# Seven block products for eight in half of an FFN's down projection, summed in device memory, with gate and up products sharing PSUM banks

## The chip, the cores and the metric

The kernel runs on one core of one Trainium2 chip, in one launch. The metric is the time of one execution on the device in microseconds (us). Three runs of the kernel before gave 1963.62, 1964.08 and 1964.83 us; the median, 1964.08 us, is the time before.

## The reference, cut to what matters

One layer of a diffusion backbone on 384 tokens (128 context, 256 latent) of width 2048, in float32. The layer's last part, where the change lies, is a dense SwiGLU FFN with a hidden width of 5632:

```
h  = rmsnorm(x, norm_pre_ffn) * (1.0 + sc2) + sh2
ff = (silu(h @ w_ffn_gate) * (h @ w_ffn_up)) @ w_ffn_down
x  = x + ga2 * rmsnorm(ff, norm_post_ffn)
```

`sc2`, `sh2` and `ga2` come from a matrix `w_ada` of the conditioning vectors ("ada" below); the last sixth of it (for `ga2`) is worked out during the FFN.

## The kernel before, in words

**Number form.** Matrix products are made in float32 quality from two parts of each operand: `hi`, the operand rounded to float32r, and `lo`, the rest. A product is three matmuls: hi x hi, hi x lo, lo x hi. A weight tile of 128 x 1024 is loaded as it is (`raw`), ACT casts it to `whi` (L1398) and DVE subtracts to get `wlo` (L1409). Four buffers of each let this run three tiles ahead of PE.

**Chunks.** The hidden width is cut into 11 chunks of 512 (4 tiles of 128). Chunk 0 of gate and up is made with plain products. From chunk 1 on, gate and up together use a block scheme (Strassen's kind) over token tiles 1 and 2 (latent) and the two halves of the width 2048: sums of blocks of `h` are made once (`left_sums`, L1297), differences of weight tiles are made by DVE as they come (L1382, L1405, L1406, L1408), and ten results per chunk, `p1` to `p7` and `q1` to `q3`, are held in PSUM. They are reached by kinds of steps, four steps (i = 0..3) to a kind: A (p1, q1), B (p5, q3), C (q3, p3), E (p6), F (p7), G (q2, p2), H (p4) (`of_kind`, L1519). A step makes two products (12 matmuls of 128x512), or one (6) in E, F and H. `evict` (L1530) copies and adds the results into SBUF with ACT and DVE, applies SiLU, and multiplies to the hidden values. In each of the first three B steps of a chunk, one token tile of the hidden values of the chunk before is transposed on PE (`turn_hid`, L1553) into a PSUM tile `ptr`; from it ACT makes `hid_hi`, DVE `hid_lo`.

**Down projection.** The hidden values of chunk c - 1 are multiplied by w_d while chunk c's gate and up products run. A D step i takes one weight tile: columns 512 n of the output (n = i // 2) and half kh = i % 2 of the chunk, for three token tiles: 18 matmuls into three PSUM banks (`pdn`). After kh = 1, `out` (L1571) adds the three banks into `psums`, a running sum of 128 x 6144 in SBUF (for chunk 0 it copies).

**Order.** `steps` (L1320) is the written order of one chunk: A0-A3, B0-B3, then four times (C, E, D of n = 0, 1), then four times (F, G, H, D of n = 2, 3). At each step `grab2` (L1419) takes the next split weight tile, starts loads (`load_more`, L1361) and splits the tile three steps on (`split_next`, L1389). Work on results waits in two lists: `now`, run at the next step, and `pend`, of which three are run per step between ACT's cast and DVE's subtraction, or all of them before a D step that needs new banks. The tiles of A and B stay in eight slots (`slots`) since E, F and H use differences of them; the tiles of C, G and D come through two `raw` buffers. SP issues all these loads, in order.

**PSUM.** Five banks (`pss`) serve gate and up, taken in turn by the ten results (`banks`, L1513). Three banks (`psm`) serve `pdn`, `ptr` and the ada work's small tiles.

**Ada work.** `ada_last` (L1430) goes a step on after some A, G and late D steps (`paced`, at a rate of 0.85): a load and two scaled adds of 512 on DVE, and at the end of each of four quarters two small PE steps.

**The end.** The last D products go into `add_last` (L1566) and a closing part that norms, scales, transposes and writes the output.

Of the kernel before, what the change touches and what calls it, by code (L numbers as in the profile page):

```python
# [11 lines left out]
F32 = mybir.dt.float32  # L12
# [8 lines left out]
P = 128  # L21
# [75 lines left out]
def tile_step(ctx: ExitStack, tc: tile.TileContext, a, o):  # L97
# [947 lines left out]
    with ExitStack() as s:  # L1045
# [234 lines left out]
        psums = [actp.tile([P, 6, 512], F32, tag=t, name="psums") for t in ("B_hi", "B_lo")]  # L1280
# [4 lines left out]

        hid = hid_of()
        s_tiles = [pe.tile([P, 8, P], F32R, tag=f"S{n}", name="S", bufs=1) for n in range(2)]
        s_tiles += [pf.tile([P, 8, P], F32R, name=f"S{n}") for n in range(2, 6)]
# [8 lines left out]
        def left_sums():  # L1297

            raw = [psums[n // 3][:, 2 * (n % 3) : 2 * (n % 3) + 2, :].rearrange("p a (b c) -> p (a b) c", c=P) for n in range(4)]
# [21 lines left out]
        steps = []  # L1321
        for c in range(1, NFC):
            steps += [("A", c, i) for i in range(4)] + [("B", c, i) for i in range(4)]
            for i in range(4):
# [10 lines left out]
        def src_of(kind, c, i):  # L1335
            if kind == "D":
                return down_src(c, i // 2, i % 2)
            return gu_src(*{"A": ("u", c, 0), "B": ("g", c, 0), "C": ("g", c, 1), "G": ("u", c, 1)}[kind], i)

        entries = [["R", 0, 0, e[0]] for e in raws]  # L1340
# [5 lines left out]
        for kind, c, i in steps:  # L1346
            e = [kind, c, i, None]
            entries.append(e)
            if kind in "CGD":
                pairs.append((e, src_of(kind, c, i)))  # L1350
        resident = [(kind, c, i) for c in range(1, NFC) for kind in "AB" for i in range(4)]
        out_now = [sum(e[3] is not None for e in entries)]
        free = set(range(8))

        def slot(x, c, i):

            return 4 * ((c + x) % 2) + i

        def load_more(kept=1):
            while pairs and out_now[0] < 2:  # L1360
                e, src = pairs.pop(0)  # L1361
                e[3] = wp.tile([P, G], F32, tag="raw", name="raw", bufs=2)
                dst = e[3]
                if e[0] == "D":
                    dst = dst.rearrange("p (i x) -> p i x", i=2)
                elif e[0] != "R":
                    dst = dst.rearrange("p (n x) -> p n x", n=FC)
                SP.dma_start(dst, src)
                out_now[0] += 1
            while kept and resident:  # L1370
                kind, c, i = resident[0]
                k = slot(kind == "B", c, i)
                if k not in free:
                    return
                free.remove(k)
                SP.dma_start(slots[k].rearrange("p (n x) -> p n x", n=FC), src_of(kind, c, i))
                resident.pop(0)
                kept -= 1

        def sum1(c, i):  # L1380
            x, y = (slots[slot(n, c, i)] for n in range(2))
            DVE.tensor_sub(x, y, x)  # L1382
# [6 lines left out]
        def split_next():  # L1389

            if not entries:
                settle_pend()
                return
            kind, c, i, raw = entries.pop(0)
            x, y = (slots[slot(n, c, i)] if kind not in "RD" else None for n in range(2))
            src = raw if kind in "RCGD" else y if kind == "F" else x
            hi, lo = (wp.tile([P, G], F32R, tag=t, name=t, bufs=4) for t in ("whi", "wlo"))
            ACT.copy(hi, src)  # L1398
            settle_pend()
            if (kind, i) == ("A", 3):  # L1400
                sum1(c, 0)
            elif kind == "B" and i < 3:
                sum1(c, i + 1)
            elif kind == "C":
                DVE.tensor_sub(x, raw, x)  # L1405
                DVE.tensor_sub(y, raw, y)  # L1406
            elif kind == "G":
                DVE.tensor_sub(x, raw, x)  # L1408
            DVE.tensor_sub(lo, src, hi.bitcast(F32))  # L1409
            if kind in "RCGD":  # L1410
                out_now[0] -= 1
            elif kind == "F":
                free.add(slot(1, c, i))
            elif kind == "H":
                free.add(slot(0, c, i))
            ready.append((hi, lo))
# [73 lines left out]
        def products(w, todo, by_tile=False):  # L1490

            order = [(x, y) for x in ((0, 1),) for y in todo] if by_tile else [((0,), y) for y in todo] + [((1,), y) for y in todo]
            for ws, (dst, stat, mov, first, last) in order:
                for w_ in ws:
                    for m in range(2):
                        for x_ in range(2 - w_):
                            PE.matmul(  # L1497
                                dst, stat[x_][m], mov(w[w_], m),
                                start=first and w_ == m == x_ == 0, stop=last and w_ == m == 1,
                            )  # L1500
# [11 lines left out]

        def banks(c):  # L1513

            for n in ("p1", "q1", "p5", "q3", "p3", "p6", "p7", "p2", "q2", "p4"):
                bank[c, n] = pss.tile([P, 512], F32, tag="side", name="pgu")
# [13 lines left out]
        def evict(c, kind):  # L1530

            B = {n: bank[c, n] for n in ("p1", "q1", "p5", "q3", "p3", "p6", "p7", "p2", "q2", "p4")}
            add, mul = DVE.tensor_add, DVE.tensor_mul
            silu = lambda x: ACT.activation(x, x, AF.Silu)
            if kind == "A":
                now.extend([lambda: ACT.copy(s1, B["p1"]), lambda: ACT.copy(sq, B["q1"])])
            elif kind == "B":
                now.append(lambda: ACT.copy(s5, B["p5"]))
            elif kind == "C":
                pend.extend([lambda: add(g0, sq, B["q3"]), lambda: add(g1, s5, B["p3"]), lambda: silu(g0)])  # L1540
            elif kind == "E":
                pend.extend([lambda: add(e2, s1, B["p6"]), lambda: add(g1, g1, e2), lambda: silu(g1)])
            elif kind == "F":
                pend.extend([lambda: add(e2, e2, B["p7"]), lambda: add(s5, s5, e2), lambda: silu(s5)])
# [5 lines left out]
            elif kind == "H":  # L1550
                pend.extend([lambda: add(e2, e2, B["p4"]), lambda: mul(s5, s5, e2)])

        def turn_hid(dst, t, pool, tag):  # L1553
# [6 lines left out]
            pend.extend([lambda: ACT.copy(hi, pt), lambda: DVE.tensor_sub(lo, pt, hi.bitcast(F32))])  # L1560

# [18 lines left out]
        pd_tiles, hid_last, x1b, done = None, None, None, 0  # L1580
        for kind, c, i in steps:
# [8 lines left out]
            if kind == "D":  # L1590
                w = grab2()
                n, kh = i // 2, i % 2
                if kh == 0:
# [5 lines left out]
                    d_live[0] = 3  # L1599
# [6 lines left out]
                if kh == 1:  # L1606
                    if not last_c:
                        for t in range(3):
                            pend.append(lambda u=unit(t, n), p=pd_tiles[t], c=c: out(u, p, c))
# [11 lines left out]
                if (c, i) == (NFC - 2, 6):  # L1621
# [4 lines left out]
                    for t in range(3):  # L1626
                        turn_hid(hid_last, t, psm, "mm")
            else:
                if kind == "A" and i == 0:
                    banks(c)  # L1630
                w = grab2()
                products(w, [(bank[c, n], two_of(stat, i), mov_gu, first and i == 0, i == 3 and last) for n, stat, first, last in of_kind[kind]])
                if i == 3:
                    evict(c, kind)
                if kind == "B" and c > 1 and i < 3:

                    turn_hid(hid, i, psm, "mm")
# [157 lines left out]
```

## Time and profile before

| | |
|---|---|
| median of three runs | 1964.08 us (1963.62 to 1964.83) |
| profiled execution | 1964.35 us, of which its span 1962.6 us |
| matmuls of L1497 into `pgu`, `pdn` (128x512) | 2640 and 1584 |
| DVE adds into `psums`, chunks 1 to 9 | 108, median 680 ns |
| loads of w_d | 88 of 512 KB, 3.6 us to landing |
| bytes read from and written to device memory | 361 MB and 17 MB, 193 GB/s over the span |

How it is read: PE is the matrix engine, PEld its weight loads, DVE, ACT and POOL the vector, scalar and GpSimd engines, SP the engine that issues DMAs. A group line gives source line, engine, operation, output<-input by the program's names, shapes, count, and then busy time, the mean of one in ns, and the idle time of that engine just before. A stretch line gives the stretch, its length, the busy time and instruction count of PE, PEld, DVE, ACT and POOL, the granted clock of PE, the DMA share and GB/s. A line of the order in time gives start, duration and instruction, and in brackets the idle time before it and what ended it. A matmul's duration holds its passage through the array, so a chain of matmuls moves on faster than the sum of their durations.

### The profile page before, as it was taken

To read this page: it belongs to the slowest core of one execution; us is meant where nothing else is said; L and a number is where in the kernel's file an instruction comes from. 1 tells how busy PE (TensorE), PEld (TensorE's weight loads), DVE (VectorE), ACT (ScalarE), POOL (GpSimd) and SP (SyncE) were. 2 spreads that over 40 slices of the span, in tenths; PEclk is the share of its full clock that TensorE was granted. 3 is DMA by queue.
4 is the path that set the end of the run, shared out by engine and by line. 5 is a ranking of instruction groups with operands and counts; after the bars stand their busy time and mean duration, and the time that the engine had idled before them with its cause. 6 is when DMAs were issued, how large, how long until landed. Compare 5 with 4: busy or idle time off the path is not lost.

```text
span 1962.6 us, 27507 instructions
## 1 busy us (share of the span) xinstructions
PE 1946.2 (99%) x10576; PEld 1725.5 (88%) x10576; DVE 1629.0 (83%) x2075; ACT 908.0 (46%) x1281; POOL 32.2 (2%) x44
## 2 busy tenths in 40 slices
PE   8999999999999999999999999999999999999998
PEld 5779999999999999999988888888888888888886
DVE  5569888879866797977789998999898989887885
ACT  4233454544345654446455444444444444444444
POOL 0000000000000000004000000000000000000001
PEclk9999999999999999999999999999999999999999
DMA  9977677767754687655345445463636263625243
GB/s 389 370 261 269 222 247 237 234 219 251 255 201 148 228 261 237 217 163 213 112 145 173 160 134 170 142 195 122 194 121 208 95 216 105 202 72 193 75 161 129
DMA packets 189411, 380.06 MB, mean 194 GB/s; under 512 B 14172, under 2 KB 112668, under 8 KB 184928
## 3 DMA queue, kind: packets, MB, share of 16 engines
q1 hardware_dynamic: 189136, 377.92, 57.4%
q8 instruction: 83, 1.36, 0.3%
q14 instruction: 48, 0.39, 0.1%
q10 hardware_dynamic: 144, 0.39, 0.1%
HBM read 361.48 MB, written 16.78 MB: 193 GB/s over the span
## 4 chain that ended last, share of the span: by engine, by line
PE 95%; DMA 2%; DVE 2%; ACT 1%; issue 0%; SPq 0%; DVEq 0%; ACTq 0%
PE pmm L258 35%; PE pgu L1497 30%; PE pdn L1497 18%; PE pv L398 3%; PE pgm L381 1%; DMA slab<-in_w_ada 1%; PE pf L996 1%; PE px L416 1%; PE pmm L1251 1%; PE ptr L1558 1%; PE po L645 1%; PE pf L997 0%; DMA raw<-in_w_br_gla 0%; DMA raw<-in_w_d 0%; PE pr L580 0%
## 5 line engine op out<-in xcount | busy, mean ns | idle before, releaser
L258 PE MATMUL pmm<-A_hi,whi 128*128 128x384 f32 x1200 | 404.3, 337 | 0.0
L258 PE MATMUL pmm<-A_hi,wlo 128*128 128x384 f32 x1200 | 401.4, 334 | 0.0
L258 PE MATMUL pmm<-A_lo,whi 128*128 128x384 f32 x1200 | 401.3, 334 | 0.0
L1398 ACT CAST whi<-u 128x1024 fp32r<-128x1024 f32 x200 | 210.7, 1053 | 285.8 <-DVE u L1382 86.2
L224 ACT CAST whi<-raw 128x1024 fp32r<-128x1024 f32 x181 | 189.7, 1051 | 188.9 <-DMA raw<-in_w_gate 63.2
L1398 ACT CAST whi<-raw 128x1024 fp32r<-128x1024 f32 x175 | 184.2, 1052 | 198.3 <-PE pgu L1497 59.9
L1409 DVE TENSOR_TENSOR wlo<-u,whi 128x1024 fp32r<-128x1024 f32 x200 | 243.9, 1220 | 33.6 <-ACT whi L1398 18.6
L225 DVE TENSOR_TENSOR wlo<-raw,whi 128x1024 fp32r<-128x1024 f32 x179 | 218.1, 1221 | 57.9 <-ACT whi L224 57.2
L1497 PE MATMUL pgu<-whi,A_hi 128*128 128x512 f32 x640 | 250.0, 391 | 0.0
L1497 PE MATMUL pgu<-whi,A_lo 128*128 128x512 f32 x640 | 249.3, 389 | 0.0
L1409 DVE TENSOR_TENSOR wlo<-raw,whi 128x1024 fp32r<-128x1024 f32 x175 | 213.3, 1219 | 33.7 <-ACT whi L1398 21.9
L258 PEld LDWEIGHTS pmm<-A_hi,whi 128*128 128x128 f32 x1200 | 225.3, 188 | 2.9 <-issue 1.4
L258 PEld LDWEIGHTS pmm<-A_lo,whi 128*128 128x128 f32 x1200 | 225.4, 188 | 0.2
L258 PEld LDWEIGHTS pmm<-A_hi,wlo 128*128 128x128 f32 x1200 | 225.3, 188 | 0.0
L572 DVE SCALAR_TENSOR_TENSOR adacc<-adaw,spad,adacc 128x1024 f32<-128x1024 f32 x180 | 222.8, 1279 | 2.6 <-DMA adaw<-in_w_ada 2.2
L1497 PE MATMUL pdn<-whi,hid_hi 128*128 128x512 f32 x480 | 186.9, 389 | 0.0
L1497 PE MATMUL pdn<-whi,hid_lo 128*128 128x512 f32 x480 | 186.8, 389 | 0.0
L1497 PE MATMUL pgu<-wlo,A_hi 128*128 128x512 f32 x640 | 184.2, 389 | 0.0
L1497 PEld LDWEIGHTS pgu<-whi,A_hi 128*128 128x128 f32 x640 | 120.1, 188 | 26.1 <-issue 0.8
L1497 PEld LDWEIGHTS pgu<-wlo,A_hi 128*128 128x128 f32 x640 | 120.1, 188 | 25.4
L1497 PEld LDWEIGHTS pgu<-whi,A_lo 128*128 128x128 f32 x640 | 120.1, 188 | 25.0
L1497 PE MATMUL pgu<-whi,S 128*128 128x512 f32 x480 | 131.1, 395 | 0.0
(367 smaller groups left out, 2763.2 us busy)
## 6 DMA issues: line engine op xcount, KB each, us to landing
adaw<-in_w_ada SPq DMA_DIRECT2D x96, 512.0 KB, 4.3
raw<-in_w_d SPq DMA_DIRECT2D x88, 512.0 KB, 3.6
slab<-in_w_ada SPq DMA_DIRECT2D x32, 1024.0 KB
raw<-in_w_gate SPq DMA_DIRECT2D x64, 512.0 KB, 4.7
raw<-in_w_g SPq DMA_DIRECT2D x48, 512.0 KB, 3.3
raw<-in_w_u SPq DMA_DIRECT2D x48, 512.0 KB, 3.3
raw<-in_w_in SPq DMA_DIRECT2D x44, 512.0 KB, 4.4
u<-in_w_u SPq DMA_DIRECT2D x40, 512.0 KB, 4.9
```

The source lines that it names most:

```text
L224: ACT.copy(hi, raw)
L225: sub = lambda: eng.tensor_sub(lo, raw, hi.bitcast(F32))
L258: PE.matmul(dst, w[wi][:, k * n + n0 : k * n + n0 + P], x[xi][:, k0 + k, :], start=first and k == 0 and j == 0, stop=last and k == kts - 1 ...
L381: PE.matmul(pgv[q : q + 32, :], spad[:, k, :], slab[k // (KT // 2)][:, k % (KT // 2), :], start=k < 4, stop=k >= KT - 4,)
L398: PE.matmul(pv[2 * t + g], hT[x_][:, kb, t * P : (t + 1) * P], w_[:, g * 512 : (g + 1) * 512], start=kb == 0 and j == 0, stop=kb == KT - 1 ...
L416: PE.matmul(px, w_[:, u * P : (u + 1) * P], hT[x_][:, kb, :], start=j == 0, stop=j == 2)
L572: DVE.scalar_tensor_tensor(acc[:, c, :], w, spad[:, k, c : c + 1], acc[:, c, :], op0=ALU.mult, op1=ALU.add,)
L645: PE.matmul(dst, w[wi], x[xi], start=first and j == 0, stop=last and j == 2)
L996: PE.matmul(pf[:, 0 : 2 * HT], w[0][:, c], x[k], start=k == 0, stop=False)
L1398: ACT.copy(hi, src)
L1409: DVE.tensor_sub(lo, src, hi.bitcast(F32))
L1497: PE.matmul(dst, stat[x_][m], mov(w[w_], m), start=first and w_ == m == x_ == 0, stop=last and w_ == m == 1,)
```

## The change

For the columns n = 0, 1 of w_d and chunks 0 to 8, the four weight blocks (two n, two kh) are multiplied with the hidden values of token tiles 1 and 2 in seven block products instead of eight; token tile 0 keeps its four products. New steps: DA (q1, p1), DB (p5, q3), DC (q3, p3), DE (p6), DF (p7), DG (q2, p2), DH (p4). DA's and DB's weight tiles stay in two new slots; DVE makes four differences of weight tiles, and three more tiles have to be split. `hid_sums` makes four sums of blocks of the hidden values with DVE, reading the transposes in PSUM, and their hi and lo parts.

The ten results are not combined in each chunk: each is a sum over chunks kept in device memory (`sums_d`), and so are the six results of n = 2, 3. `to_sums` copies a bank with ACT into one of four SBUF buffers; SP writes it for chunk 0, and an accumulating DMA of POOL adds it for chunks 1 to 8. In the last chunk they are loaded back (`sums_back`, `sums_rest`), and nine adds (`sums_join`) combine them in `psums`. Chunk 9's down projection and the last one are as before.

The space of `psums` holds, until then, the two slots, the buffers and the hidden sums.

Gate and up: the ten results become chains in five fixed banks. Q is q1, copied after A and added to in B and C; X is p1 (A), then p6 (E), p7 (F) and p4 (H) added on top; Z is p5 (B), then p3 (C). X and Z change places from chunk to chunk. `evict` copies some sums out on the way and has seven adds or products to make instead of twelve. The order of a chunk is now A, B, four times (C, E, D-step), four times (F, G, D-step), four times (H, D-step), with eleven D-steps: D4, D5, DA, DB, DC, D6, D7, DE, DF, DG, DH.

```diff
+        sums_d = dram.tile([16, P, 512], F32, name="sums_d")
...
+            if c < LAST:
+                dd = iter([("D", c - 1, 4), ("D", c - 1, 5), ("DA", c - 1, 0), ("DB", c - 1, 0), ("DC", c - 1, 0),
+                           ("D", c - 1, 6), ("D", c - 1, 7)] + [("D" + k, c - 1, 0) for k in "EFGH"])
...
             for i in range(4):
-                steps += [("C", c, i), ("E", c, i), ("D", c - 1, i)]
+                steps += [("C", c, i), ("E", c, i)] + more()
             for i in range(4):
-                steps += [("F", c, i), ("G", c, i), ("H", c, i)] + ([("D", c - 1, 4 + i)] if c < NFC - 1 or i < 2 else [])
+                steps += [("F", c, i), ("G", c, i)] + more()
+            for i in range(4):
+                steps += [("H", c, i)] + more()
...
+            if kind == "DA":
+                DVE.tensor_sub(x, y, x)
...
         of_kind = {
-            "A": (("p1", Hx(1, 0), True, True), ("q1", Hx(0, 0), True, True)),
-            "B": (("p5", S1, True, True), ("q3", Hx(0, 0), True, False)),
-            "C": (("q3", Hx(0, 8), False, True), ("p3", S4, True, True)),
-            "E": (("p6", S2, True, True),),
-            "F": (("p7", S3, True, True),),
-            "G": (("q2", Hx(0, 8), True, True), ("p2", Hx(1, 8), True, True)),
-            "H": (("p4", Hx(2, 8), True, True),),
+            "A": (("Q", Hx(0, 0), True), ("X", Hx(1, 0), True)),
+            "B": (("Z", S1, True), ("Q", Hx(0, 0), False)),
+            "C": (("Q", Hx(0, 8), False), ("Z", S4, False)),
+            "E": (("X", S2, False),),
+            "F": (("X", S3, False),),
+            "G": (("q2", Hx(0, 8), True), ("p2", Hx(1, 8), True)),
+            "H": (("X", Hx(2, 8), False),),
         }
...
             elif kind == "C":
-                pend.extend([lambda: add(g0, sq, B["q3"]), lambda: add(g1, s5, B["p3"]), lambda: silu(g0)])
+                now.append(lambda: silu(g0, B["Q"]))
             elif kind == "E":
-                pend.extend([lambda: add(e2, s1, B["p6"]), lambda: add(g1, g1, e2), lambda: silu(g1)])
+                now.append(lambda: ACT.copy(e2, B["X"]))
+                pend.extend([lambda: add(g1, e2, B["Z"]), lambda: silu(g1)])
             elif kind == "F":
-                pend.extend([lambda: add(e2, e2, B["p7"]), lambda: add(s5, s5, e2), lambda: silu(s5)])
+                pend.extend([lambda: add(s5, s5, B["X"]), lambda: silu(s5)])
...
+        def hid_sums(h1, h2):
+
+            r, (hi, lo) = dt["raw"], dt["S"]
+            add, sub = DVE.tensor_add, DVE.tensor_sub
+            return [
+                lambda: ACT.copy(r[:, 3], h2[:, 0:2]),
+                lambda: add(r[:, 0], r[:, 3], h2[:, 2:4]), lambda: sub(r[:, 1], r[:, 0], h1[:, 0:2]),
+                lambda: sub(r[:, 2], h1[:, 2:4], r[:, 1]), lambda: sub(r[:, 3], h1[:, 0:2], r[:, 3]),
+                lambda: ACT.copy(hi, r), lambda: sub(lo, r, hi.bitcast(F32)),
+            ]
+        of_d = {
+            "DA": lambda: (("q1", Hd(0, 0), True, True), ("p1", Hd(1, 0), True, True)),
+            "DB": lambda: (("p5", Sd(0), True, True), ("q3", Hd(0, 0), True, False)),
+            "DC": lambda: (("q3", Hd(0, 1), False, True), ("p3", Sd(2), True, True)),
+            "DE": lambda: (("p6", Sd(1), True, True),),
+            "DF": lambda: (("p7", Sd(3), True, True),),
+            "DG": lambda: (("q2", Hd(0, 1), True, True), ("p2", Hd(1, 1), True, True)),
+            "DH": lambda: (("p4", Hd(2, 1), True, True),),
+        }
+        def to_sums(k, p, c):
+
+            u = dt["out"][turn[0] % 4]
+            turn[0] += 1
+            ACT.copy(u, p)
+            if c == 0:
+                SP.dma_start(sums_d[k], u)
+            else:
+                POOL.dma_start(sums_d[k], u, accum_op=ALU.add)
+            d_live[0] -= 1
...
-        def out(u, p, c):
-            if c == 0:
-                ACT.copy(u, p)
-            else:
-                DVE.tensor_add(u, u, p)
+        def out(u, p):
+            DVE.tensor_add(u, u, p)
             d_live[0] -= 1
...
+                    if c < LAST and i == 3:
+                        if c == 1:
+                            f = dt["full"]
+                            pend.append(lambda: DVE.tensor_add(f, hid[0][:, :, P:T].bitcast(F32), hid[1][:, :, P:T].bitcast(F32)))
+                            pend.extend(hid_sums(f[:, :, 0:P], f[:, :, P:]))
+                        else:
+                            pend.extend(hid_sums(*hid_pt[1:]))
```

More of the change, by code (lines that the diff above doesn't have):

```diff
@@ L1380, in sum1 @@
         def sum1(c, i):
[L1381 removed]
+            x, y = (slots[slot(n, "A", c, i)] for n in range(2))
             DVE.tensor_sub(x, y, x)
@@ L1492, in products @@
             order = [(x, y) for x in ((0, 1),) for y in todo] if by_tile else [((0,), y) for y in todo] + [((1,), y) for y in todo]
-            for ws, (dst, stat, mov, first, last) in order:
+            for ws, (dst, stat, mov, first, last, *more) in order:
                 for w_ in ws:
@@ L1627, in tile_step @@
                         turn_hid(hid_last, t, psm, "mm")
-            else:
-                if kind == "A" and i == 0:
-                    banks(c)
+            elif kind[0] == "D":
+                w = grab2()
+                while pend:
+                    pend.pop(0)()
+                todo = []
+                for n, stat, first, last in of_d[kind]():
+                    if first:
+                        d_bank[n] = psm.tile([P, 512], F32, tag="mm", name="pds")
+                        d_live[0] += 1
+                    todo.append((d_bank[n], stat, mov_d, first, last))
+                    if last:
+                        pend.append(lambda k=PROD.index(n), p=d_bank[n], c=c: to_sums(k, p, c))
+                products(w, todo, by_tile=kind in ("DB", "DC"))
+            else:
@@ L1631, in tile_step @@
                 w = grab2()
-                products(w, [(bank[c, n], two_of(stat, i), mov_gu, first and i == 0, i == 3 and last) for n, stat, first, last in of_kind[kind]])
+                if kind == "H" and i == 0:
+                    while pend:
+                        pend.pop(0)()
+                B = banks(c)
+                products(
+                    w, [(B[n], two_of(stat, i), mov_gu, first and i == 0, i == 3, not first) for n, stat, first in of_kind[kind]],
+                    by_tile=(kind, i) in (("A", 3), ("B", 0), ("B", 3), ("C", 0)),
+                )
```

144 lines of the change are left out of this document (105 added, 39 removed).

## The prediction

> **What bounds the kernel now.** I read the page first, then the busy time by stretch for the part that the change touches (the FFN chunks, 1062 to 1912 us), then the chain of work there.
>
> ```profile
> span 1962.6 us, 27507 instructions
> PE 1946.2 (99%) x10576; PEld 1725.5 (88%) x10576; DVE 1629.0 (83%) x2075; ACT 908.0 (46%) x1281; POOL 32.2 (2%) x44
> ```
> ```profile
> 1062.00:1912.00 850.00, 850.00 (x3858) 701.82 (x3857) 763.44 (x833) 383.94 (x414) 0.00 (x0) 1.00 0.45 148
> ```
> ```profile
> 1212.70:1307.10 94.40, 94.40 (x424) 78.14 (x423) 91.40 (x103) 42.56 (x46) 0.00 (x0) 1.00 0.51 166
> 1307.10:1401.60 94.50, 94.50 (x437) 77.76 (x436) 85.35 (x96) 42.07 (x47) 0.00 (x0) 1.00 0.47 152
> ```
> ```profile
> 1401.59 5.44 PE pgu L1497 x24
> 1407.03 4.08 PE pdn L1497 x18
> ```
>
> In these stretches PE (first busy figure) fills all 850 us at granted clock 1.00; a list of PE's waits there is empty. So a matmul saved there is time saved, unless a wait comes up. The chain gives the price: 24 matmuls of 128x512 in 5.44 us, 18 in 4.08 us, **0.2267 us each**. But a chunk takes 94.4 us and DVE (third figure) is busy 85 to 91 of them: it keeps ahead of PE by little. A new wait for DVE is therefore what I look for.
>
> **The change, part by part.** All from the profiled execution (1964.35 us, 1.75 above its span, 0.27 above the median 1964.08).
>
> *Matmuls.* For each of chunks 0 to 8 the columns n = 0, 1 of w_d take 11 products of 6 matmuls (7 blocks for token tiles 1 and 2, 4 for tile 0) instead of 12. 9 x 6 = 54 fewer, which the built order confirms (9998 to 9944): 54 x 0.2267 = **-12.2 us**. The gate/up products stay 44 per chunk; sharing banks moves no matmul.
>
> *DVE's queue.* Its prices, from the start of one instruction to the next while it never idles (chunk 4's tiles B and C, the fourth column on is the instruction; then one evaluation chain; then a narrow one):
>
> ```profile
> 1268.76 1.40 DVE L1440 SCALAR_TENSOR_TENSOR acc<-w,spad,acc 128x512 f32<-128x512 f32 x2
> 1270.09 1.21 DVE L1409 TENSOR_TENSOR wlo<-u,whi 128x1024 fp32r<-128x1024 f32 x1
> 1271.22 0.68 DVE L1560 TENSOR_TENSOR hid_lo<-ptr,hid_hi 128x512 fp32r<-128x512 f32 x1
> 1271.82 1.21 DVE L1405 TENSOR_TENSOR u<-raw,u 128x1024 f32<-128x1024 f32 x1
> 1272.95 1.21 DVE L1406 TENSOR_TENSOR u<-raw,u 128x1024 f32<-128x1024 f32 x1
> 1274.09 1.22 DVE L1409 TENSOR_TENSOR wlo<-raw,whi 128x1024 fp32r<-128x1024 f32 x1
> 1275.22 0.68 DVE L1560 TENSOR_TENSOR hid_lo<-ptr,hid_hi 128x512 fp32r<-128x512 f32 x1
> ```
> ```profile
> 1339.91 0.68 DVE L1547 TENSOR_TENSOR ep<-ep,pgu 128x512 f32<-128x512 f32 x1
> 1340.63 0.69 DVE L1547 TENSOR_TENSOR ep<-ep,ep 128x512 f32<-128x512 f32 x1
> 1341.24 0.68 DVE L1548 TENSOR_TENSOR ep<-ep,pgu 128x512 f32<-128x512 f32 x1
> 1341.84 1.22 DVE L1409 TENSOR_TENSOR wlo<-u,whi 128x1024 fp32r<-128x1024 f32 x1
> ```
> ```profile
> L345 DVE TENSOR_TENSOR wlo<-xraw,whi 128x256 fp32r<-128x256 f32 x16 | 6.7, 419 | 0.0
> ```
>
> 1024 wide: 1.135. 512 wide: 0.60, and 0.72 where the next needs its result. A scaled-add step of the ada work (two instructions): 1.33. 256 wide: duration 0.42, by the same steps 0.34, and 0.46 before a dependent one (estimates from these rows). Per chunk go 12 psums adds and 5 gate/up adds (17 x 0.61 = 10.3); come 3 more weight splits, 4 weight differences, the low part of the hidden sums (8 x 1.135 = 9.1) and 4 narrow sums (1.6): +0.4, as good as nothing in total. ACT gains some 13 us on 42 of 93 and has room. It is the places that count, and two are tight.
>
> *Place 1: a PSUM bank held longer.* The three transposes of hid fill all three banks of the small pool. Before, `hid_lo` freed each. Now `hid_sums` reads two of them, and the third token tile of the first down product (D4, n = 2) waits for its last subtraction. In the built order DVE has, after `lo` of tile C0: hid_lo, lo(E0), hid_lo, lo(D4), two narrow sums, two differences and lo for C1, two narrow sums: those last free the bank. Behind the waiting matmul stands all of PE. ACT and the load of C1's weights enter this path:
>
> ```profile
> 1268.75 1.04 ACT L1398 CAST whi<-raw 128x1024 fp32r<-128x1024 f32 x1
> 1269.69 0.58 ACT L1560 CAST hid_hi<-ptr 128x512 fp32r<-128x512 f32 x1
> ...
> 1278.66 1.05 ACT L1398 CAST whi<-raw 128x1024 fp32r<-128x1024 f32 x1 [2.06 <-DMA raw<-in_w_g]
> ```
> ```profile
> 1267.79 1.18 PE L1497 MATMUL pgu<-whi,S 128*128 128x512 f32 x4
> ...
> 1271.00 1.17 PE L1497 MATMUL pgu<-whi,S 128*128 128x512 f32 x4
> ```
>
> These are ACT's and PE's rows of the same chunk; B2 and B3 start at 1267.79 and 1271.00, so a B tile with its transposes is 3.21. Let x be when lo(C0) ends, counted from B3's start. C1's raw buffer is free then; its load comes in and ACT starts at x + 3.35 (1274.09 + 1.22 to 1278.66). ACT casts (0.94 to its next start), copies a quarter (0.36, estimated from 512 wide in 0.58 and 1024 in 1.05), handoff 0.06: first narrow sum at x + 4.7. Then 0.46 + 0.34 + 3 x 1.135 + 0.34 + 0.42: the bank is free at **x + 9.7**. PE is there after B3, C0, E0 (2.72 + 2.72 + 1.36) and 8 matmuls (1.81): **8.6**. No wait needs x below -1.1.
>
> What is x? Count DVE's queue from tile F3 of the chunk before (its start = 0; the weights of tile t are split while PE runs tile t - 3). From C0 to D7 it has 50 to 51 us of such work for 53 of PE's, so I let it start there without lag, idle until D7 frees a buffer: lo(H0), the add for F, then lo(DF) at 2.8, when ACT's cast for it is done. From there until lo(C0) it never waits: 13 more lo besides DF's and 7 differences, 21 x 1.135 = 23.8; G's four, H's one and one hid_lo of 512, 3.7; k ada steps in A and one in G3, 1.33 each. With k = 3: 2.8 + 23.8 + 3.7 + 5.3 + 1.2 = 36.8. PE needs 72 matmuls (16.3), four A tiles (10.9), three B tiles (9.6) to B3's start: 36.8. So **x = 0**, wait 1.1; with k = 4, x = 1.3, wait 2.4. The built order has k = 3 in chunks 2, 3, 6, 7, 8; k = 4 in 4 and 5; none in 9, where x reaches -1.1. Chunk 1 takes the sums from SBUF, so it has no such wait. 5 x 1.1 + 2 x 2.4 = **+10.3 us**; ends: 0 if the path is 2.4 shorter than counted, 20 if each link is late by the 1.3 of one more step.
>
> *Place 2: the short tiles* DE, H0, DF, H1, DG stand in a row, 1.36 each, DG 2.72, without an 18-matmul tile between them. lo(H1) is ready at 2.8 + 1.135 + 1.33 + 1.93 + 1.22 = 8.4, needed at 8.16 + 4 matmuls = 9.1. lo(DG): 11.3, needed at 11.3. No reserve. Taken 0.3 in the 7 chunks with an ada step in G3, and 0.4 more in the three that finish an ada quarter there: **+3.3**; ends 0 and 9 (1.3 in each, if ACT's cast for DF waits for the three copies out of PSUM ahead of it).
>
> *Sums in device memory.* 16 copies of 512 per chunk, SP writes them for chunk 0, POOL adds them for 1 to 8. The trace has no accumulating DMA; nearest rows:
>
> ```profile
> w<-in_w_ada SPq DMA_DIRECT2D x64, 256.0 KB, 2.5
> gates_d<-gz SPq DMA_DIRECT2D x32, 192.0 KB, 4.0
> ```
>
> Low end 2.5 (one read of the size). High end a read and then a write, 2.5 + 4.0 x 256/192 = 7.8. I take 5, nearer the write. Four buffers take turns; the nearest reuse is q1/p1 after D5's first unit, 6.7 us later, and ACT then has some 3 us until G0's casts are needed: hidden up to about 10 us, so +0. Traffic grows by 9 x 16 x 0.26 MB written and 8/9 of it read, 71 MB over 850 us or 84 GB/s beside 148; no stretch of the page with 389 GB/s stood still for that.
>
> *Gate/up chains.* Q, X, Z must be copied before PE writes on. Q after A3: X's 6 and Z's 6 matmuls lie between (2.7 us) and ACT needs about 0.7; Z at C0 the same; X at F0 has tile DB (2.7); X at H0 has G3 and DE (4.1) for an add of 0.7 that is free by 2.2. Nothing, unless DVE lags by over 3 us there. *Last chunk.* 10 loads and 9 adds (5.6) more on DVE, in a chunk without ada work; 3 us of lag at most, against 8 us of lead: nothing. SP's waiting writes in chunk 0: up to 1 us behind raw loads, hidden by the second raw buffer.
>
> **Sum:** 1964.35 - 12.2 + 10.3 + 3.3 + 0 = **1966** (rounded up by 0.2).
>
> **Rivals.**
> - *The bank wait does not bind.* DVE would have to reach lo(C0) over a microsecond sooner than counted. For it: before, no DVE lag ever reached PE. Against it: the same queue in before ended lo(C0) 4.3 us after B3 began (1275.31 against 1271.00), later than I count. Then 1964.35 - 12.2 + 0 to 3: 1952 to 1955.
> - *DVE paces both places*: lag is 1 us more throughout, place 1 costs 18, place 2 9: 1964.35 - 12.2 + 27 = 1979. For it: 91.4 of 94.4 busy in the chunk ahead of the quoted one. Against: DVE idles just before H0, where the lag starts anew.
> - *The accumulating writes are late* (slower). If one takes over 10 us from copy to completion, ACT's next copy into that buffer waits, at p1 and at p7, and whi for G0 and H3 behind it. Each microsecond over 10 costs up to 2 x 8 = 16 us: at 12 us, 1998. Against: the high end above is 7.8. The Trainium skill's page "SBUF — State Buffer", section "Who interferes with whom", says that a DMA issued from GpSimd starves for descriptors while DVE holds the shared ports, which copies and tensor_scalar can do and tensor_tensor cannot. By that rule it is not late here, since nearly all of DVE's rows are TENSOR_TENSOR; no run here shows it yet, and it lowers this rival's chance somewhat.
>
> The change does what it says, by the counts of the built order.
>
> **How the numbers follow.** Forecast, place 1 gives the gain back: 0.58, 1960 to 1974. No wait: 0.15. DVE paces: 0.14. Late writes: 0.13. What a measurement of this kernel can tell from no change is 0.2%, 3.9 us: 1960.4 to 1968.3. Of the forecast 0.04 is below that, 0.35 within, 0.19 above. Faster 0.15 + 0.04 = 0.19; same 0.35; slower 0.19 + 0.14 + 0.13 = 0.46. Range: leaving out half of "no wait" and most of the late writes, 1955 to 1984.
>
> **What would show it.** PE's waits in chunks 2 to 8: `pdn` waiting for DVE's narrow subtraction (about 1.1 and 2.4 us, none in 1 and 9) means place 1; `pds` or `pgu` waiting for wlo in H1 and DG means place 2; ACT's copies to `spare` and `dw` ended by a DMA means late writes. A chunk of 93.0 us without waits of PE would prove me wrong.

## The result, and the profile after

The changed kernel takes **1993.38 us** (median of four runs, 1990.84 to 1994.06) against 1964.45 us of the kernel before in the same session: 1.0145 times as long, 95% interval 1.0128 to 1.0163. The prediction was 1966, its range ended at 1984. The profiled execution took 1990.84 us, the fastest of the four; its span grew by 26.4 us (the medians are 28.9 apart).

The page of the changed kernel (engines' busy time, then the queue of POOL's DMAs with packets, MB and share of the 16 DMA engines):

```profile
span 1989.0 us, 28106 instructions
PE 1947.8 (98%) x10522; PEld 1717.5 (86%) x10522; DVE 1639.6 (82%) x2047; ACT 1005.6 (51%) x1468; POOL 144.4 (7%) x172
...
q0 software_dynamic: 18432, 33.56, 10.9%
```

PE makes 54 matmuls fewer (10522 after 10576) and is busy 1.6 us longer, in a span 26.4 us longer. So it now waits, and some of its work is slower. PE's waits (what waits, for what; us in total, times, the longest) are what the kernel before did not have in the FFN:

```profile
PE pdn L1530 <- DVE dw L1606: 12.2, 7, 2.8
PE pgu L1530 <- DVE wlo L1440: 6.5, 4, 3.0
...
PE pdn L1530 <- DVE hidE L1596: 2.6, 1, 2.6
PE pgu L1530 <- ACT whi L1429: 1.7, 1, 1.7
...
PE pds L1530 <- DVE wlo L1440: 0.9, 3, 0.3
```

The first row is place 1 of the prediction, in chunks 2 to 8 once each, each time at the ninth matmul of D4, the third token tile. Place 2 (the short tiles) are three of the four `wlo` waits of `pgu`, in H1 of chunks 1, 5 and 7, and the `wlo` waits of `pds`, in DG: 6.4 us in six waits. The fourth `wlo` wait (1.1 us, C3 of chunk 1) and the one for `whi` (1.7 us, G1 of chunk 9) lie at places that the prediction did not name. `hidE` is a wait at the very end that it did not have either.

**Slower work.** PE's order in time around place 1 of chunk 5 (start, duration, instruction, wait in brackets), and then the stretches with the granted clock (third figure from the right):

```profile
1384.26 0.39 PE L1530 MATMUL pdn<-whi,hid_lo 128*128 128x512 f32 x1
1387.33 0.50 PE L1530 MATMUL pdn<-whi,hid_hi 128*128 128x512 f32 x1 [2.68 <-DVE dw L1606]
...
1388.69 2.77 PE L1530 MATMUL pdn<-wlo,hid_hi 128*128 128x512 f32 x6
1391.25 0.45 PE L1530 MATMUL pgu<-whi,A_hi 128*128 128x512 f32 x1
```
```profile
1383.00:1385.00 2.00, 1.65 (x8) 1.03 (x6) 2.00 (x3) 0.56 (x1) 0.00 (x0) 1.00 0.21 81
1387.00:1389.00 2.00, 1.68 (x5) 1.41 (x6) 2.00 (x3) 1.70 (x2) 0.00 (x0) 0.74 0.60 170
1389.00:1391.00 2.00, 2.00 (x6) 1.54 (x6) 2.00 (x3) 0.67 (x2) 0.00 (x0) 0.50 0.26 92
1391.00:1395.00 4.00, 4.00 (x19) 3.27 (x18) 4.00 (x5) 1.74 (x2) 0.00 (x0) 0.96 0.63 197
```

Behind the wait of 2.68 us the clock falls to 0.50. Six matmuls take 1391.25 - 1388.69 = 2.56 us, 0.43 each instead of 0.2267. The stretch costs 1.6 us on top of the wait, and a further 0.3 goes with any wait in leaving and entering the chain (1384.26 to 1387.33 is 3.07 for 0.23 of work and 2.68 of waiting, and as much again in the matmuls behind it).

**The account of the 26.4 us.** Matmuls: -12.2. Place 1: waits 12.2, seven starts of 0.3, half clock behind the waits of 2.8 and 2.7 us, 1.6 each: +17.5. The end, from the first transpose of the last hidden values to the last matmul: 1929.65 to 1982.51 now, 1907.13 to 1956.10 before, +3.9. The remainder is +17.2, of which 4.9 fall ahead of chunk 2's transposes (0.4 of them ahead of the FFN), 4.9 in chunk 7 and 3.1 in chunk 9. Place 2 has 9.8 of it: waits 6.4, six starts 1.8, half clock behind the wait of 3.0 us in chunk 7, 1.6. The waits in C3, G1 and two short ones for `ep` in B0, with their starts, have another 4.3; 3.1 stay unassigned.

**Where DVE is late.** In the stretch 1062 to 1840 us DVE's waits, and the loads of raw tiles of w_u (KB each, median us to landing):

```profile
DVE u L1439 <- DMA raw<-in_w_u: 27.7, 20, 5.2
```
```profile
raw<-in_w_u SPq DMA_DIRECT2D x32, 512.0 KB, 5.3
```

In the kernel before, the same loads land in 3.7 us, in the same stretch, and DVE has no such wait:

```profile
raw<-in_w_u SPq DMA_DIRECT2D x32, 512.0 KB, 3.7
```

And one chain of place 2, the longest wait of PE there (3.0 us, chunk 7), as the chain of work that ended last has it:

```profile
1629.57 6.52 DMA w<-in_w_ada
...
1636.18 1.41 DVE acc L1473 x2
1637.60 0.61 DVE ep L1583
...
1639.52 1.15 DVE wlo L1440
...
1640.71 1.22 PE pgu L1530 x2
```

A load of ada weights takes 6.5 us here (the median of the stretch is 5.1, after 2.5 before), DVE stands at the ada step that wants it, and `wlo` of an H tile is behind that step. Two theories follow. **Places**: single instructions stand badly in the queues of ACT and DVE. **Traffic**: the accumulating writes make loads late, and DVE with them, everywhere.

### The profile page after: what moved, and what is told of

The parts are those of the page before. It is cut to its first block, busy times and chain, and to the rows that moved or that the text cites. A ratio compares the mean times of both kernels' runs of the same rounds, so it can differ in the third digit from the quotient of the medians.

```text
span 1989.0 us, 28106 instructions
## 1 busy us (share of the span) xinstructions
PE 1947.8 (98%) x10522; PEld 1717.5 (86%) x10522; DVE 1639.6 (82%) x2047; ACT 1005.6 (51%) x1468; POOL 144.4 (7%) x172
## 3 DMA queue, kind: packets, MB, share of 16 engines
q0 software_dynamic: 18432, 33.56, 10.9%
## 4 chain that ended last, share of the span: by engine, by line
PE 74%; DVE 12%; DMA 7%; issue 4%; ACT 2%; SPq 0%; POOL 0%; DVEq 0%; ACTq 0%; POOLq 0%
PE pmm L258 34%; PE pgu L1530 16%; PE pdn L1530 8%; DVE wlo L1440 5%; PE pds L1530 4%; PE pv L398 3%; DVE acc L1473 2%; DMA raw<-in_w_u 1%; PE pgm L381 1%; DMA raw<-in_w_g 1%; ACT whi L1429 1%; DMA raw<-in_w_d 1%; DMA slab<-in_w_ada 1%; PE pf L996 1%; PE px L416 1%
## 5 line engine op out<-in xcount | busy, mean ns | idle before, releaser
L224 ACT CAST whi<-raw 128x1024 fp32r<-128x1024 f32 x181 | 189.8, 1051 | 177.4 <-DMA raw<-in_w_gate 61.2
L1429 ACT CAST whi<-raw 128x1024 fp32r<-128x1024 f32 x157 | 165.0, 1051 | 206.7 <-DMA raw<-in_w_u 61.8
L225 DVE TENSOR_TENSOR wlo<-raw,whi 128x1024 fp32r<-128x1024 f32 x179 | 218.0, 1221 | 55.8 <-ACT whi L224 54.2
L1440 DVE TENSOR_TENSOR wlo<-raw,whi 128x1024 fp32r<-128x1024 f32 x157 | 191.7, 1221 | 42.5 <-ACT whi L1429 38.0
L1530 PE MATMUL pgu<-whi,S 128*128 128x512 f32 x400 | 119.5, 396 | 0.0
L1530 PE MATMUL pdn<-whi,hid_hi 128*128 128x512 f32 x264 | 104.7, 397 | 12.3 <-DVE dw L1606 12.2
L1636 POOL DMA_DIRECT2D sums_d<-spare x64 | 58.7, 992 | 664.6 <-ACT spare L1632 474.8
```

What stands on the lines that cost most here:

```text
L224: ACT.copy(hi, raw)
L225: sub = lambda: eng.tensor_sub(lo, raw, hi.bitcast(F32))
L1530: PE.matmul(dst, stat[x_][m], mov(w[w_], m), start=first and w_ == m == x_ == 0, stop=last and w_ == m == 1, skip_group_check=any(more),)
L1636: POOL.dma_start(sums_d[k], u, accum_op=ALU.add)
```

## The experiments

Each ratio is to the kernel before, run on the same chip in the same session, with its 95% interval.

### Theory against theory: e1 to e4

**e1, the sums first.** The work of `hid_sums` is issued at once, ahead of ACT's cast for C1, instead of three items per step behind it:

```diff
                             pend.extend(hid_sums(*hid_pt[1:]))
+                            while len(pend) > 2:
+                                pend.pop(0)()
```

> The edit runs the copy and the four narrow sums of hid_sums ahead of ACT's cast and DVE's differences for tile C1, so the banks come free earlier. Theory 'places' (the loss comes from where single instructions stand in the queues of ACT and DVE; the changed kernel's trace shows the copy behind a cast that waits 2.7 us for C1's weights): PE's waits of pdn for the narrow subtraction, 12.2 us in 7, go, and the half clock after them; 17.6 us counted at this place, so 1993.4 falls to 1973 to 1979. Theory 'traffic' (the accumulating writes slow the weight loads, DVE runs late everywhere): the lateness turns up at the next tight place, 1982 to 1990.

Measured: 1982.23 us, 1.0091 (1.0074 to 1.0109). In PE's waits the row of `pdn` for `dw` is gone; the others stay, and the one at the end too:

```profile
PE pgu L1530 <- DVE wlo L1440: 7.2, 5, 2.0
...
PE pdn L1530 <- DVE hidE L1596: 2.8, 2, 2.3
```

Place 1 is a matter of the queue's order, as "places" has it. It gave 11 us instead of 17.5: PE's place-2 waits grew a little, as "traffic" expected of a DVE that is late for another reason too. By its time alone, 1982.23, the run stands at the low end of what "traffic" gave (1982 to 1990), above what "places" gave; it is the row that is gone that shows the cause of place 1.

**e2, the short tiles apart.**

```diff
-                dd = iter([("D", c - 1, 4), ("D", c - 1, 5), ("DA", c - 1, 0), ("DB", c - 1, 0), ("DC", c - 1, 0),
-                           ("D", c - 1, 6), ("D", c - 1, 7)] + [("D" + k, c - 1, 0) for k in "EFGH"])
+                dd = iter([("D", c - 1, 4), ("D", c - 1, 5), ("DA", c - 1, 0), ("DB", c - 1, 0)]
+                          + [("D" + k, c - 1, 0) for k in "CEFG"] + [("D", c - 1, 6), ("D", c - 1, 7), ("DH", c - 1, 0)])
```

> The edit moves the two 18-matmul tiles D6, D7 from the F and G tiles to among the H tiles, and DE, DF, DG from among the H tiles to among F and G, so that no run of short tiles DE, H0, DF, H1, DG is left. Theory 'places': most of the 16.5 us counted at place 2 goes, 1977 to 1983. Theory 'traffic': the loads are as late as before and PE waits for other tiles instead, 1988 to 1996.

Measured: 1996.28 us, 1.0161 (1.0146 to 1.0176). No gain, but not for the reason expected of "traffic": PE's waits show a new one.

```profile
PE pdn L1530 <- ACT dw L1632: 14.3, 9, 2.4
PE pdn L1530 <- DVE dw L1606: 5.6, 5, 1.9
```

D6 wants all three small banks right behind DG, whose two are still being copied out by ACT. PE's waits for `wlo` shrank to one of 1.0 us, but the edit put new bank waits in their place, and DVE can catch up during those; so it does not tell what the short tiles themselves cost.

**e3 and e4, no accumulating writes, and plain ones.** In `to_sums`, for chunks 1 to 8, e3 drops the line that starts the DMA; e4 writes instead:

```diff
-                POOL.dma_start(sums_d[k], u, accum_op=ALU.add)
+                POOL.dma_start(sums_d[k], u)
```

> Leaves out the adding in device memory for chunks 1 to 8: the copies out of PSUM stay, the 128 accumulating writes are not issued. Theory 'traffic': weight loads land as fast as in the kernel before (3.3 to 3.7 us for 512 KB), place 2 falls to the 3 us of the prediction, place 1 to about 10, 1970 to 1977. Theory 'places': nothing but the queues' order matters, 1989 to 1994.

> The same 128 writes from the same queue without adding (the sums over chunks are left out). If it is the adding (read and write of the target, 10.9% of the DMA engines' time for 33.6 MB) that slows the loads: 1972 to 1980. If it is the bytes written or the queue of descriptors that POOL feeds: 1987 to 1994. Theory 'places': 1989 to 1994.

Measured: e3 1980.37 us, 1.0077 (1.0060 to 1.0094); e4 1981.89 us, 1.0089 (1.0074 to 1.0104). PE's waits in e3, then DVE's for the raw tiles of w_u and their loads in the stretch 1062 to 1840:

```profile
PE pdn L1530 <- DVE dw L1606: 12.6, 7, 2.7
...
PE pgu L1530 <- DVE wlo L1440: 2.6, 2, 1.6
```
```profile
DVE u L1439 <- DMA raw<-in_w_u: 7.2, 11, 1.6
```
```profile
raw<-in_w_u SPq DMA_DIRECT2D x32, 512.0 KB, 3.9
```

Place 1 is untouched (12.6 in 7 waits, after 12.2 in 7) and place 2 is left in chunk 1 alone, where SP writes the sums and nothing is added yet. So e1 and e3 split the loss along the two theories: **place 1 is order; place 2 from chunk 2 on needs the accumulating writes.** (e8 and e9 below show that it needs the ada steps where they stand as well.) The times of e3 and e4, 1980 and 1982, lie between the two theories' ranges, above the 1970 to 1977 that "traffic" gave for e3: place 1 did not shrink with the writes, as had been expected.

e4 tells which property it is. The same 33.56 MB from the same queue, without adding:

```profile
q0 software_dynamic: 10240, 33.56, 4.7%
```

1.5 us are between e3 and e4, 11.5 between e4 and the changed kernel: in this order of steps the adding costs, not the writing. With it, the same bytes took 18432 packets instead of 10240 and 10.9% of the engines' time instead of 4.7%.

### Part by part: e5 to e7

**e5, the chains alone.** The kernel before, with `of_kind`, `banks`, `evict` and `products` of the changed kernel and H behind F and G:

```diff
-                steps += [("F", c, i), ("G", c, i), ("H", c, i)] + ([("D", c - 1, 4 + i)] if c < NFC - 1 or i < 2 else [])
+                steps += [("F", c, i), ("G", c, i)] + ([("D", c - 1, 4 + i // 2)] if i % 2 == 0 else [])
+            for i in range(4):
+                steps += [("H", c, i)] + ([("D", c - 1, 6 + i // 2)] if c < NFC - 1 and i % 2 == 0 else [])
```

> The kernel before with one part of the change alone: gate and up products share five PSUM banks along chains, H tiles stand behind F and G (D4 to D7 among them); the down projection keeps its eight products and its sums in SBUF. If the chains cost nothing, as predicted: 1960 to 1967. If evictions between the links of a chain make PE wait (the changed kernel has 0.4 us of PE's waits for ACT's copy out of pgu in all), or H tiles in a row do it as in the changed kernel: over 1969.

Measured: 1970.44 us, 1.0032 (1.0020 to 1.0045), in the second expectation (over 1969). But the loss is at one place, as PE's waits say:

```profile
PE pdn L1499 <- DVE hidE L1565: 3.0, 2, 2.5
```

From one chunk's first transpose to the next's it is 94.9 and 93.9 to 94.3 us in turn, 94.9 and 93.9 in the kernel before: in the chunks the chains cost 0.3 us in all. At the end, from the transposes to the last matmul, it is 53.2 instead of 49.0. So the loss at the end comes with this part of the change. In it the last H tiles, of 6 matmuls each, stand in a row ahead of D6 and D7; that this row makes the loss, and not the shared banks, is likely but was not run apart.

**e6, the copies of the last hid first.** ACT in the changed kernel, at that place:

```profile
1935.51 1.04 ACT L1429 CAST whi<-raw 128x1024 fp32r<-128x1024 f32 x1 [4.36 <-DMA raw<-in_w_d]
1936.46 1.55 ACT L1596 CAST hidE<-ptr 128x512 fp32r<-128x512 f32 x3
```

The transposes had ended by 1930.9. The three copies wait 5.5 us behind a cast that waits for its load. The order is not new: in the kernel before they stood behind such a cast too, but that waited 2.15 us, not 4.36, and PE did not wait for `hidE`.

```diff
                         turn_hid(hid_last, t, psm, "mm")
+                    while pend:
+                        pend.pop(0)()
```

> The changed kernel, with ACT's three copies of the last hid (hidE) ahead of its cast of the next w_d tile instead of behind it. If the 3.9 us lost at the end come from the copies standing behind a cast that waits 4.4 us for its load: PE's wait for hidE (2.6 us) and the half clock behind it go, 4 us less than the changed kernel: 1987 to 1991. If the loads of the last tiles themselves are late: PE waits for wlo instead, no gain, 1991 to 1995.

Measured: 1985.59 us, 1.0110 (1.0095 to 1.0125). This is below the first expectation. The wait for `hidE` is gone, and the end takes 49.1 us. That is 3.8 us; the median fell by 7.8. The two profiled executions are only 5.3 apart, and 1.2 of the difference lies ahead of the FFN. The other 2.5 of the median are what the changed kernel's profiled execution lay below its own median; no trace shows their cause.

**e7, place 1 made longer.**

```diff
+                lambda: sub(r[:, 2], h1[:, 2:4], r[:, 1]), lambda: sub(r[:, 2], h1[:, 2:4], r[:, 1]),
                 lambda: ACT.copy(hi, r), lambda: sub(lo, r, hi.bitcast(F32)),
```

> The changed kernel with one of the narrow sums of hid_sums done three times: the banks come free about 2.0 us later in the chunks of place 1 (two more narrow sums, and the split between them). PE's waits there go from 1.3 to 2.8 up to 3.3 to 4.8. If only the wait itself costs: 7 x 2.0 us more, 2006 to 2009. If a wait over some 2 to 2.5 us also halves the granted clock for about 3 us behind it (1.6 us lost each, seen so far behind the waits of 2.6 to 3.0 us and behind none of 1.8 or less): five more such stretches, 2014 to 2018.

One difference is worked out three times, so the banks come free later. Measured: 2016.29 us, 1.0261 (1.0246 to 1.0277), in the second expectation: 22.9 more than the changed kernel, where the waits alone (first row) grew by 14.2. The matmuls behind these eight waits lost 14.5 us, those behind the seven of the changed kernel 4.2. The stretches of 3 us right behind three of them, of 3.19, 2.30 and 1.92 us, show the clock at 0.50, 0.58 and 1.00:

```profile
PE pdn L1530 <- DVE dw L1607: 26.4, 8, 4.8
```
```profile
1097.28:1100.28 3.00, 3.00 (x7) 2.42 (x8) 1.94 (x2) 1.87 (x2) 0.00 (x0) 0.50 0.19 66
1700.24:1703.24 3.00, 3.00 (x8) 2.38 (x9) 1.94 (x2) 2.07 (x2) 0.00 (x0) 0.58 0.19 67
1797.65:1800.65 3.00, 3.00 (x13) 2.50 (x14) 1.94 (x2) 2.08 (x2) 0.00 (x0) 1.00 0.19 65
```

So a wait of some length costs more than itself, as the second expectation has it.

### What is left: e8 to e12

**e8** joins e1 and e6 and takes the ada steps off the G tiles, D6 and D7:

```diff
-                if kind in "AG":
+                if kind == "A":
...
-                if not last_c and i >= 4:
+                if not last_c and i in (4, 5):
...
+                if kind == "DB":
+                    step(ada)
...
-        rate[0] = 0.85
+        rate[0] = 1.2
```

> e1 and the edit of the last hid together, and the steps of the ada work taken from the G tiles and from D6, D7 to DB (1.2 steps for each A tile, D4, D5 and DB). If place 2 is DVE's queue there (three ada steps, 4 us, among the splits of G3 to DG, begun late behind a load): 1982 less 4 for the end and 8 to 15 for place 2, 1962 to 1971. If the accumulating writes alone make place 2, whatever DVE has in its queue: 1976 to 1980.

Measured: 1979.54 us, 1.0081 (1.0061 to 1.0100). The time is in the second expectation, but not for its reason. The `wlo` waits shrank to 3.0 us, 2.2 of it in C3 of chunk 1; in H1 and DG 1.1 us are left, with the adding still there. And a new wait came, most of it in B0 of chunks 6 and 8, for copies of A's results. PE's waits, DVE and ACT there:

```profile
PE pgu L1530 <- ACT ep L1571: 8.3, 4, 3.2
```
```profile
1446.47 2.73 DVE L1473 SCALAR_TENSOR_TENSOR acc<-w,spad,acc 128x512 f32<-128x512 f32 x4
...
1453.66 1.41 DVE L1473 SCALAR_TENSOR_TENSOR acc<-w,spad,acc 128x512 f32<-128x512 f32 x2 [2.18 <-DMA w<-in_w_ada]
```
```profile
1456.32 1.04 ACT L1429 CAST whi<-u 128x1024 fp32r<-128x1024 f32 x1 [4.82 <-DVE u L1412]
1457.27 1.07 ACT L1571 COPY ep<-pgu 128x512 f32<-128x512 f32 x2
```

Two ada steps fell together (x4), the next one's load was not there, DVE's difference for a B tile came late, ACT's cast waited for it, and the copies of Q and X stood behind that cast: a copy behind a waiting cast a third time, though this cast waits for DVE and not for a load.

**e9** keeps e1 and e6 and sets at most one ada step to a tile: A, D4 to D7 and DB, rate 0.95. **e11** is e9 with `grab2(kept=1)`. **e10** joins e1, e6 and e3, so it leaves out the adding. **e12** is e9 without D7's step, rate 1.0.

> Like e8 (sums first, copies of the last hid first), but at most one step of the ada work at a call: 0.95 steps for each A tile, D4 to D7 and DB. In e8 two steps in a row in A0 delayed DVE's difference for a B tile, ACT's cast of it, and ACT's copies of Q and X behind that cast (two waits of PE of 3.2 us). If place 2 and those are DVE's queue being filled at a bad moment: 1966 to 1974. If late loads alone decide: 1976 to 1981, as e8.

> Sums first, copies of the last hid first, and no accumulating writes (the adding in device memory for chunks 1 to 8 is left out). If the three causes are all there is and add up: the matmuls' 12.2 less than before, and some 4 for the waits in chunk 1 that no experiment removed: 1954 to 1960. If they overlap or hide another wait: 1961 to 1970.

> e9 with at most one load of resident weights started per tile instead of two (512 KB each, 5 to 12 us to land beside the accumulating writes), so that fewer of them stand ahead of the loads of raw and of the ada weights, which are wanted at once. If the loads collide in bursts: 2 to 6 less than e9. If the traffic as a whole decides, or resident weights then come late: as e9 or some us more.

> e9 with D7's step of the ada work, the last ahead of the short tiles, given to the other places (one step for each A tile, D4, D5, D6 and DB). In e9 some 5 us of small waits of PE are left in the short tiles, behind that step and loads of raw that land late. If the step is what is left of place 2: 1960 to 1963, faster than the kernel before by up to 0.2%. If the late loads are: 1964 to 1967, as e9. The floor is e10 without the adding, 1958.9.

| | median us | ratio | interval |
|---|---|---|---|
| e9 | 1965.53 | 1.0008 | 0.9999 to 1.0017 |
| e10 | 1958.87 | 0.9972 | 0.9963 to 0.9982 |
| e11 | 1965.99 | 1.0011 | 1.0002 to 1.0020 |
| e12 | 1963.31 | 0.9998 | 0.9989 to 1.0007 |

e9 is just below its first expectation: the ada steps' places decided most of what was left, 14 us between e8 and e9 for the same work. e11 made no difference: it is not the pairs of resident loads. e10 is within its first expectation: with the three causes out, PE's waits in the chunks are nearly those of chunk 1 alone (the two longest rows of the stretch 1000 to 1840):

```profile
PE pgu L1530 <- DVE wlo L1440: 2.4, 2, 1.6
PE pgu L1530 <- DVE ep L1580: 1.8, 1, 1.8
```

Some chunks take 92.57 us from first transpose to first transpose, after 93.94: 1.37 us, the 6 matmuls of 0.2267. So the saved matmuls are saved in full where PE does not wait. The account is not closed by this: of the 12.2 us, e10's median keeps 5.4 and its profiled execution, the second slowest of ten, 2.7. In that one 6.9 are lost ahead of chunk 2's transposes, where the waits stand, and 3.0 in the chunks behind, in which the list shows no wait over 0.2 us.

e12, the best that was found with the sums complete, lies between its two expectations and can be told neither from e9 nor from the kernel before. The adding costs less here than it did: 11.5 us between e4 and the changed kernel, 6.7 between e10 and e9, which also differ in the ada steps. So the adding and the places of the ada steps work together; e9's places without the adding were not run.

## Why the prediction was wrong, point by point

- **Matmuls** (-12.2): right; the chunks of e10 in which PE does not wait show 1.37 each.
- **DVE's queue** (+0.4 a chunk in all): right; DVE's busy time grew by 10.6 us over the whole span, with the last chunk's nine adds in it.
- **Place 1** (+10.3): mechanism, count and waits right, the sum too small. Foreseen were seven waits, 1.1 or 2.4 us, none in chunk 9; found seven, 12.2 us, with 2.76 and 2.68 in chunks 4 and 5 and 0.65 to 1.79 in the five others. The path can be read off chunk 5. DVE, then ACT:

```profile
1375.74 1.22 DVE L1440 TENSOR_TENSOR wlo<-raw,whi 128x1024 fp32r<-128x1024 f32 x1
...
1382.32 0.88 DVE L1605 TENSOR_TENSOR dw<-dw,ptr 128x256 f32<-128x256 f32 x2 [1.90 <-ACT dw L1604]
...
1386.52 0.75 DVE L1606 TENSOR_TENSOR dw<-ptr,dw 128x256 f32<-128x256 f32 x2
```
```profile
1380.97 1.05 ACT L1429 CAST whi<-raw 128x1024 fp32r<-128x1024 f32 x1 [2.72 <-DMA raw<-in_w_g]
1381.92 0.36 ACT L1604 COPY dw<-ptr 128x256 f32<-128x256 f32 x1
```

  B3 starts at 1375.74, so x = 1.22 (foreseen 1.3); ACT starts at x + 4.0 (foreseen 3.35); the bank is free at x + 10.3 (9.7). What failed is the step that took a wait to cost its own length: 0.3 more per wait and 1.6 of half clock behind the two long ones make 17.5, still inside the ends of 0 and 20. The order itself could have been questioned: the copy at 1381.92 needed only transposes that were done by 1376, and stood behind the cast.
- **Place 2** (+3.3, ends 0 and 9): wrong, 9.8, above the upper end. Another 4.3 came at places put at nothing (C3, G1, B0), and 3.1 stay unassigned. The step that failed took DVE to start into the short tiles without lag, idle and with its loads there; DVE waits for raw tiles of w_u instead, and for ada weights. Without the accumulating writes (e3) it is the waits of chunk 1 that remain, and without ada steps in G3 and D7 (e8) 1.1 us of the waits in H1 and DG.
- **Sums in device memory** (+0): the copies were never held up by a late write. The median landings were 6.7 and 7.7 us, taken as 5 with a bound of 7.8, the longest 9.0 and 10.4, and none of ACT's waits is ended by one of these writes. So the rival "late writes" did not come about. Nor does a row show a queue starved of descriptors: in e4 plain writes of the same queue landed in 3.2 and 5.2 us. (The Trainium skill's page "SBUF — State Buffer", section "Who interferes with whom", expects that only beside DVE's copies and tensor_scalar; with 6.7 and 7.7 us to landing the trace does not speak against it.) The step that failed is the one on traffic, which weighed bytes (71 MB at 84 GB/s) and took other loads not to notice: the added writes took 2.3 times the engine time of plain ones (10.9% against 4.7%), and the raw loads of w_u went from 3.7 to 5.3 us. This was the term that was missing: 11.5 us between e4 and the changed kernel.
- **Gate/up chains** (nothing): right in the chunks (e5). **Last chunk** (nothing): wrong by 3.9, for ACT's copies behind a cast.
- **Rivals**: "late writes" was nearest in time (1998 at 12 us a write), by luck: no copy waited for a write. "DVE paces both places" (1979) was right that lag was more; but at place 1 x was as counted, and the lag at place 2 came from late loads and from ada steps that waited for them.

## What to carry to other kernels

Where an engine takes its queue in order, ask of each copy that frees a bank what stands ahead of it: here three times a short copy stood behind a cast that waited, twice for a load and once for DVE, with its own input long there. In the first two (e1, e6) issuing the copy first took the wait away; the third went with the ada steps spread (e9). Price a transfer that adds in device memory by the time it takes of the DMA engines, not by its bytes, and look for loads that are wanted at once beside it. In this kernel a stall of PE of over about 2 us is to be priced at its length plus some 2 us, a shorter one at its length plus 0.3.

## What the runs showed of the hardware that was not expected

**The clock behind a stall.** Over the changed kernel and seven of the experiments (e1 to e4, e6 to e8) PE has 91 waits of more than 0.6 us in the FFN. Behind none of the 57 of up to 1.92 us did the granted clock leave 1.00 in the next 3 us; it fell behind 16 of 22 from 2.04 to 2.71 us, and behind all 12 from 2.74 us on. The matmuls behind those lost mostly 1.7 us (1.5 to 3.0), some 1.6 of it by the clock. The half clock lasts 3.41 us, in five cases 6.83 (the wait of chunk 5 above; just before and behind this stretch the clock is 1.00):

```profile
1387.94:1391.35 3.41, 3.41 (x10) 2.67 (x9) 3.41 (x5) 2.08 (x3) 0.00 (x0) 0.50 0.45 141
```

Within a kernel such stretches start whole multiples of 3.413 us apart (1288.96 and 1387.94 in the changed kernel, 29 of them), so the time can be laid out in windows of that length. That settles why some waits of over 2 us escape. From full rate, the clock fell behind every window in which PE was idle for 1.91 us or more, behind one of four with 1.83 to 1.87 us, and behind none with less; the six waits that escaped lay across the border of two windows. In the five stretches of 6.83 us the first window at half rate had 0.5 to 2.7 us of idle time itself.

The Trainium skill's page "TensorE: Matmul & The Clock Gate", section "What's actually happening", has the clock halved after an idle window of about 3.4 us, in windows that run free. The trace agrees with the two states and with the windows (3.41 us). It differs on the gap to avoid, which the section "HAM oscillation — how this bites in real kernels" puts above about 3.4 us: here a wait of 2.04 us was enough, and 1.91 us of idle time in one window.

**Writes that add.** In the changed kernel sixteen per chunk of 256 KB slowed loads that SP issues on another queue (raw tiles of w_u, 5.3 us after 3.7); with plain writes of the same size these land in 3.9 us, as without any (e4, e3). The adding alone does not set it: in e12, with the adding, their median is 3.7 us again, though DVE still waits 18.2 us for them in the stretch 1062 to 1840, after 7.2 in e3. Why among the raw tiles those of w_u suffer most, and why the ada weights' loads stay slow without the adding (4.6 us after 2.5 before, in e3), is open.
